# First block of a two-layer product on one core: halves of k for two strips, and four strips ahead of the second half of x

## The chip, the cores and the metric

The kernel runs on one core of a Trainium2 chip. The metric is the device time of one execution in microseconds (us), the median of several runs. The engines are named as the profile names them: PE (matrix multiply), PEld (its weight load), DVE, ACT, POOL and SP. POOL, ACT and SP also start transfers (DMA).

## The reference

```python
def reference(x, w1, b1, w2):          # x 16x512x768, w1 768x3072, b1 3072, w2 3072x768
    y = np.matmul(x, w1) + b1
    y = np.maximum(y, 0)
    return np.matmul(y, w2)
```

The 16x512 rows of x are one matrix of 8192 rows.

## The kernel before

The rows of x are cut into 8 blocks of 1024, and the hidden width of 3072 into two halves. The 16 pairs of a block and a half are the iterations. Each iteration has a first stage (x by w1, bias, relu, giving y) and a second stage (y by w2, added into the output). Fifteen iterations use a fast product scheme that forms sums of tiles of x, w1, y and w2 on DVE and needs fewer products. Its first stages are line 1091 and its second stages line 1219.

The very first first stage can't do that, because w1 and x are still on their way. It is written plainly in `first_block` (line 1021) with products from `plain` (line 983), whose matmuls are line 995. It works on six strips of w1. A strip is 256 columns with all 768 rows, so six matrices of 128x256; it is held as two halves of k, each with three of the six. The name `strip` counts 0 to 5, `j` picks one of a strip's two column tiles of 128, and `m` picks the first or the second 512 rows of the block. So there are 24 products `plain(strip, j, m)`. With `parts=2` a product is done as two groups of 256 rows (`n` is 0 or 1), with six matmuls of 256 columns each; with `parts=1` it is six matmuls of 512 columns. `split=True` cuts work further into the two halves of k, for n = 0 only. Each product fills one PSUM bank, and ACT evicts it with bias and relu into y (line 1003).

The first 512 rows come as four plain transfers, two each from SP and ACT. PE turns them (line 935, fp32), and DVE and ACT copy the results into x (lines 943 and 941). Everything else comes by POOL's queue, which also converts to 16 bits. The order is written out in `prologue` (line 717): strip 0 in two halves of k, strips 1 and 2 whole (`load_strip`, line 688, transfer on line 694), the second 512 rows of x in two transfers of 256 rows (`load_x`, line 710, transfer on line 715), strips 3 to 5, twelve pieces of w2 (line 700), and the first half of the next block. The second 512 rows are turned by PE in two groups of two tiles (`turns(0, 1)`, `turns(2, 3)`), again on line 935.

The order of PE's work is that of the program text. All other engines' instructions are put in order by a planner (`Graph.run`, line 390), which simulates the whole kernel with a table of costs. `presets` (line 739) tells it when each loaded piece is taken to have landed. The table changes no wait: on the chip each instruction waits for its real operands. It does change the order in which DVE, ACT, POOL and SP take their instructions, and which PSUM bank a product gets. `Reg("ps", leaves=...)` tells the planner in which state a bank is left.

Of the kernel before, what the change touches and what calls it, by code (L numbers as in the profile page):

```python
# [129 lines left out]
LAST_PARTS = ((0, 0, 384, "ACT", "SP"), (1, 0, 384, "ACT", "ACT"))  # L130
LAST_DIRECT = (0, 1, 2, 3, 4, 5, 7)
LAST_POOL = (0, 1, 3)

X_FUSE = (3,)
Y_FUSE = (8, 12, 18, 20)
# [148 lines left out]
class Graph:  # L284
# [23 lines left out]
    def add(self, engine, ns, fn, reads=(), writes=(), due=None, lat=0.0, after=(), idle=False, dma=0.0,  # L308
            early=0.0, spare=0.0, port=False):
        t = Task()  # L310
        t.n, t.engine, t.ns, t.fn, t.lat, t.due, t.idle = (
            len(self.tasks), engine, max(ns / 1000.0 - self.OVER[engine], 0.0), fn, lat, due, idle)
        t.succ, t.ready, t.end, t.start, t.dma, t.early = [], 0.0, None, None, dma, early
        t.spare, t.port = spare, port
        deps = set(after)
        for key in reads:
            w = self.writer.get(key)
            if w is not None:
                deps.add(w)
        for key in writes:  # L320
            w = self.writer.get(key)
            if w is not None:
                deps.add(w)
            deps.update(self.readers.get(key, ()))
        for key in reads:
            self.readers.setdefault(key, []).append(t)
        for key in writes:
            self.writer[key] = t
            self.readers[key] = []
        t.deps = deps  # L330
        t.waits = len(deps)
        for d in deps:
            d.succ.append(t)
        t.regs = list(dict.fromkeys(k for k in (*reads, *writes) if isinstance(k, Reg)))
        for r in t.regs:
            r.left += 1
        t.pe = None
        if engine == "PE":
            t.pe = self.npe
            self.npe += 1  # L340
            self.last_pe = t
        self.tasks.append(t)
        return t
# [250 lines left out]
class Fast:  # L594
# [122 lines left out]
    def prologue(self):  # L717
        nc = self.nc
        for s in range(4):
            (nc.sync, nc.scalar)[s % 2].dma_start(out=self.s[:, s],  # L720
                                                  in_=self.xf[s * P:(s + 1) * P, :])
            if s == 1:
                self.load_bias()
        self.constants()
        self.load_strip(self.v1, 0, 0, 0, 2)
        self.load_strip(self.v1, 0, 0, 1)
        self.load_strip(self.v1, 0, 0, 2)
        self.load_x(0, 1, 2)
        for h in range(3):
            self.load_strip(self.v1, 0, 1, h)  # L730
        for q in range(4):
            for h in range(3):
                self.load_w2(self.v2, 0, h, q)
        self.load_x(1, 0)
        for _ in range(9):
            nc.tensor.matmul(self.ps[:, 7, 0:P], lhsT=self.ones, rhs=self.ones, start=True,
                             stop=True)

    def presets(self):
        g = self.g  # L740
        for t, at in enumerate((9.3, 11.3, 13.3, 19.9, 21.8, 23.8)):
            for k in range(2):
                g.preset(("w1", t // 3, 2 * (t % 3) + k), at - (0 if t or k else 0.9))
        for q in range(4):
            for h in range(3):
                for n in range(2):
                    g.preset(("w2", 2 * q + n, h), 24.8 + 3 * q + h)
        for s in range(4):
            g.preset(("xn", 4 + s), 15.2 if s < 2 else 17.2)
            g.preset(("xn", s), 39.5)  # L750
            g.preset(("rows", s), (5.3, 5.3, 7.2, 7.2)[s])
        g.preset("b1_rows", 6.0)
# [229 lines left out]

    def plain(self, strip, j, m, parts=1, split=False):
        gi, h = divmod(strip, 3)
        ps = Reg("ps", leaves=2 if parts == 1 else 0)
        nc = self.nc

        def product(n, k2s):
            cols = slice(n * self.QM, (n + 1) * self.QM) if parts == 2 else slice(0, 512)
            for k2 in k2s:  # L990
                for k in range(3):
                    a = 4 * m + k2
                    rhs = (self.x[:, a:a + 3:2, k, :] if parts == 1
                           else self.x[:, a + 2 * n, k, :])
                    nc.tensor.matmul(self.ps[:, ps.at[0], cols],  # L995
                                     lhsT=self.v1[:, gi, 2 * h + k2, k, j * P:(j + 1) * P],
                                     rhs=rhs, start=(k2 == 0 and k == 0),
                                     stop=(k2 == 1 and k == 2), skip_group_check=True)

        def evict():  # L1000
            n = 4 * h + 2 * gi + j
            i = 8 * m + 2 * gi + j
            nc.scalar.activation(
                out=self.y[:, i:i + 5:4, h * self.QM:(h + 1) * self.QM],
                in_=self.ps[:, ps.at[0], :].rearrange("p (a m) -> p a m", a=2),
                func=ACTF.Relu, bias=self.b1y[:, n:n + 1])

        def add(n, k2s):
            rows = (0, 1) if parts == 1 else (n,)
            self.g.add("PE", 650 * len(k2s) // parts, lambda: product(n, k2s),  # L1010
                       reads=[("x", 4 * m + 2 * r + k2, q) for r in rows for k2 in k2s
                              for q in range(2)] + [("w1", gi, 2 * h + k) for k in k2s],
                       writes=[ps])
        for n in range(parts):
            for k2s in ((0,), (1,)) if split and n == 0 else ((0, 1),):
                add(n, k2s)
                yield
        self.g.add("ACT", 692, evict, reads=[ps, "b1y"],
                   writes=[("y", (2 * m + r) * 4 + 2 * gi + j, h) for r in range(2)])

    def first_block(self):
        for s in range(4):
            self.add_transpose_first(0, s)
            if s == 1:
                tables = self.add_bias()
        tables(self.g.tasks[-2:])

        def turns(*tiles):
            for s in tiles:
                self.add_transpose_first(1, s)  # L1030

        def run(*products):
            for p in products:
                for _ in p:
                    pass

        a, b = [self.plain(0, j, 0, 2, True) for j in range(2)]
        for p in (a, b, a, b):
            next(p)
        run(a, b, *(self.plain(1, j, 0, 2) for j in range(2)), self.plain(2, 0, 0, 2))  # L1040
        turns(0, 1)
        run(self.plain(2, 1, 0, 2))
        late = [self.plain(strip, j, 1, 2) for strip, j in ((0, 0), (0, 1), (1, 0))]
        next(late[0])
        turns(2, 3)
        for p in late[1:]:
            next(p)
        run(*late, *(self.plain(strip, j, 1, 2) for strip, j in ((1, 1), (2, 0), (2, 1))))
        run(*(self.plain(strip, j, m) for strip in (3, 4, 5) for m in range(2) for j in range(2)))

    def y_keys(self, slot):
        return [("y", slot, h) for h in range(3)]
# [145 lines left out]
    def add_second(self, it):  # L1198
# [67 lines left out]
        def store(to, reg, plain):  # L1266
            out, rows = sum_of(reg), self.rows_of(it, to)
            if plain:
                nc.sync.dma_start(out=rows, in_=out)
            else:  # L1270
                nc.gpsimd.dma_start(out=rows, in_=out, accum_op=ALU.add)  # L1271
# [14 lines left out]
        def prior_task(t):  # L1286
            _, _, u, b, _, to, _ = SECOND_OPS[t]
            e, ns = ("POOL", 2400) if t in LAST_POOL else ("DVE", 955)
            if e == "POOL" and (t in LAST_HALVES or t in taken_by):
# [12 lines left out]
        for kind, n in steps:  # L1302
# [97 lines left out]
            if what == "out":  # L1400
                plain = c == 0 and n not in apart or direct
                self.g.add("SP" if plain else "POOL", 100 if plain else 1375,
                           lambda to=to, dest=dest, plain=plain: store(to, dest, plain),
                           reads=[dest], writes=[("out", self.block(it), to)],
                           lat=3.5 if direct else 9.0,
                           dma=1.09 if direct else 1.2 if plain else 2.45)
# [192 lines left out]
```

## Time and profile before

| | us |
|---|---|
| median of 3 runs | 847.02 |
| lowest and highest | 846.86 and 847.36 |
| the profiled execution | 847.05 |
| its span, first to last instruction | 845.4 |
| PE busy in that span | 839.2 |

The profile is of one execution. Times within it count from the span's start. Matmuls are pipelined: the length given for one reaches past the start of the next one, so the pace is read from how long a row of many takes. An engine's busy time is the union of its instructions. "Idle before" with an arrow names what ended the wait. The chain of work that ended last is followed back from the last instruction.

### The profile page before, as it was taken

To read this page: it belongs to the slowest core of one execution; us is meant where nothing else is said; L and a number is where in the kernel's file an instruction comes from. 1 tells how busy PE (TensorE), PEld (TensorE's weight loads), DVE (VectorE), ACT (ScalarE), POOL (GpSimd) and SP (SyncE) were. 2 spreads that over 40 slices of the span, in tenths; PEclk is the share of its full clock that TensorE was granted. 3 is DMA by queue.
4 is the path that set the end of the run, shared out by engine and by line. 5 is a ranking of instruction groups with operands and counts; after the bars stand their busy time and mean duration, and the time that the engine had idled before them with its cause. 6 is when DMAs were issued, how large, how long until landed. Compare 5 with 4: busy or idle time off the path is not lost.

```text
span 845.4 us, 16819 instructions
## 1 busy us (share of the span) xinstructions
PE 839.2 (99%) x6383; PEld 625.7 (74%) x6383; DVE 736.2 (87%) x1229; ACT 567.3 (67%) x1199; POOL 171.7 (20%) x185
## 2 busy tenths in 40 slices
PE   9999999999999999999999999999999999999997
PEld 8568778686786867768687686877868678686874
DVE  5899988969889697988999979798896979979787
ACT  4866876779677684856858568766757666456462
POOL 6210011102011010010030503224041230501303
PEclk9999999999999999999999999999999999999999
DMA  9997498978988678594893977979799797986926
GB/s 211 205 178 186 85 223 110 170 178 132 216 114 154 165 132 189 102 212 153 237 176 66 196 122 121 189 108 175 119 137 148 117 174 113 145 136 76 178 85 169
DMA packets 171111, 128.93 MB, mean 153 GB/s; under 512 B 93948, under 2 KB 169492, under 8 KB 171028
## 3 DMA queue, kind: packets, MB, share of 16 engines
q0 software_dynamic: 56576, 68.82, 53.2%
q1 hardware_dynamic: 113984, 58.02, 29.1%
q8 instruction: 50, 0.82, 0.4%
q10 hardware_dynamic: 468, 1.00, 0.3%
q14 instruction: 33, 0.27, 0.1%
HBM read 73.54 MB, written 69.21 MB: 169 GB/s over the span
## 4 chain that ended last, share of the span: by engine, by line
PE 98%; DMA 1%; POOL 0%; ACT 0%; DVE 0%; issue 0%; POOLq 0%; DVEq 0%; ACTq 0%
PE ps L1219 48%; PE ps L1091 47%; PE ps L995 4%; DMA v<-in_w_dram 1%; PE ps L935 0%; ACT s L1230 0%; POOL v L694 0%; DVE s L1236 0%; POOL ident masks.py:199 0%; POOL ident L667 0%; POOL high L679 0%; POOL low L680 0%; POOL ident masks.py:197 0%; PE ps L1417 0%; PE ps L1428 0%
## 5 line engine op out<-in xcount | busy, mean ns | idle before, releaser
L1219 PE MATMUL ps<-v,y 128*128 128x384 f16 x2496 | 408.2, 326 | 0.0
L1091 PE MATMUL ps<-x,v 128*128 128x256 f16 x3600 | 395.6, 273 | 0.0
L1091 PEld LDWEIGHTS <-v 128*128 128x128 f16 x3600 | 352.3, 98 | 42.2
L1219 PEld LDWEIGHTS <-y 128*128 128x128 f16 x2496 | 244.2, 98 | 159.9
L1230 ACT ACTIVATE s<-ps 128x384 f32<-128x384 f32 (+1 forms) x245 | 153.1, 643 | 125.2 <-PE ps L1219 118.9
L1063 DVE TENSOR_TENSOR y<-y 128x768 f16<-128x768 f16 (+1 forms) x384 | 219.4, 619 | 2.6
L1134 DVE CUSTOM_DVE_ANT_0 y<-ps,s 128x512 f16<-128x512 f32 x240 | 156.0, 686 | 52.8 <-ACT s L1131 39.8
L1271 POOL DMA_DIRECT2D out_dram<-s x78 | 93.8, 1453 | 146.2 <-ACT s L1230 91.6
L1131 ACT ACTIVATE s<-ps,bt 128x256 f32<-128x256 f32 x180 | 75.2, 469 | 62.8 <-PE ps L1091 56.5
L838 DVE TENSOR_TENSOR x<-x 128x768 f16<-128x768 f16 (+1 forms) x210 | 113.6, 579 | 1.2
L1131 ACT ACTIVATE y<-ps,bt 128x256 f16<-128x256 f32 x180 | 69.4, 485 | 10.8 <-PE ps L1091 10.8
L1230 ACT ACTIVATE ps<-ps 128x384 f32<-128x384 f32 (+1 forms) x143 | 67.0, 507 | 6.6 <-PE ps L1219 2.8
L1236 DVE TENSOR_TENSOR s<-ps,s 128x768 f32<-128x768 f32 x74 | 70.6, 954 | 0.9
L715 POOL DMA_DIRECT2D xn<-in_x_dram x30 | 25.9, 864 | 211.8 <-DMA x<-xn 100.9
L1236 DVE TENSOR_TENSOR s<-s,ps 128x768 f32<-128x768 f32 x60 | 57.1, 952 | 2.1
L777 ACT ACTIVATE junk<-xn 128x768 f16<-128x768 f16 x64 | 53.9, 843 | 0.3
L1274 POOL DMA_DIRECT2D out_dram<-s x15 | 17.8, 1184 | 169.3 <-ACT s L1230 157.6
L1131 ACT ACTIVATE ps<-ps,bt 128x256 f32<-128x256 f32 x60 | 26.7, 445 | 32.4 <-PE ps L1091 31.4
L1127 ACT ACTIVATE ps<-ps 128x512 f32<-128x512 f32 x60 | 35.3, 588 | 4.4 <-DVE y L1134 3.5
L1142 DVE TENSOR_TENSOR s<-s,ps 128x512 f32<-128x512 f32 x30 | 20.6, 686 | 17.8 <-PE ps L1091 17.8
L995 PE MATMUL ps<-x,v 128*128 128x256 f16 (+1 forms) x216 | 32.0, 308 | 0.2 <-DMA v<-in_w_dram 0.2
L1137 DVE SCALAR_TENSOR_TENSOR s<-ps,bt,s 128x256 f32<-128x256 f32 x60 | 26.1, 476 | 4.4 <-PE ps L1091 4.4
(61 smaller groups left out, 310.7 us busy)
## 6 DMA issues: line engine op xcount, KB each, us to landing
out_dram<-s POOLq DMA_DIRECT2D x93, 384.0 KB, 8.8
out_dram<-s SPq DMA_DIRECT2D x69, 384.0 KB, 7.1
xn<-in_x_dram POOLq DMA_DIRECT2D x28, 768.0 KB, 9.9
v<-in_w_dram POOLq DMA_DIRECT2D x14, 192.0 KB, 8.2
x<-out_dram SPq DMA_DIRECT2D x14, 192.0 KB, 2.4
w1d<-in_w_dram POOLq DMA_DIRECT2D x6, 384.0 KB, 6.4
w2d<-in_w_dram POOLq DMA_DIRECT2D x12, 192.0 KB, 5.0
v<-w1d SPq DMA_DIRECT2D x12, 192.0 KB, 4.7
```

Of the source, the lines that this page charges most:

```text
L777: self.nc.scalar.activation(out=self.junk, in_=self.xn[:, s, :], func=ACTF.Square, accum_out=self.stat[:, self.stat_at["x"] + i:][:, 0:1])
L838: self.nc.vector.tensor_tensor(out=self.two(x, out), in0=self.two(x, in0), in1=self.two(x, in1), op=ALU.add if sign > 0 else ALU.subtract)
L995: nc.tensor.matmul(self.ps[:, ps.at[0], cols], lhsT=self.v1[:, gi, 2 * h + k2, k, j * P:(j + 1) * P], rhs=rhs, start=(k2 == 0 and k == 0), ...
L1063: self.nc.vector.tensor_tensor(out=self.two(self.y, out), in0=self.two(self.y, in0), in1=self.two(self.y, in1), op=ALU.add if sign > 0 els ...
L1091: nc.tensor.matmul(self.ps[:, at, j * self.QM:(j + 1) * self.QM], lhsT=self.v1[:, gi, self.w1s[c][gi][FIRST_V[p]], k, j * P:(j + 1) * P], ...
L1127: nc.scalar.activation(out=out, in_=ps, scale=float(a), func=func if kind == "out" else ACTF.Copy)
L1131: nc.scalar.activation(out=out[:, j], in_=ps[:, j], func=func, scale=float(a), bias=beta(j))
L1134: nc.vector._custom_dve(TENSOR_ADD_SAT, out=out, in0=ps, in1=s, s0=F_MAX, s1=0.0)
L1219: nc.tensor.matmul(self.ps[:, bank[ch].at[j], 0:NH], lhsT=self.y[:, ys[SECOND_U[p]], m0:m0 + P], rhs=self.v2[:, slot[SECOND_V[p]], h, :], ...
L1230: nc.scalar.activation(out=out, in_=ps, func=ACTF.Copy, scale=float(a))
L1236: engine.tensor_tensor(out=out, in0=in0, in1=in1, op=ALU.add if a == b else ALU.subtract)
L1271: nc.gpsimd.dma_start(out=rows, in_=out, accum_op=ALU.add)
```

## The change

Strip 1 is now loaded in two halves of k, as strip 0 was. Strips 2 and 3 follow whole, and only then the second 512 rows of x; strips 4 and 5 come after them. That is one transfer more in all.

On the first 512 rows PE now works strips 0 and 1 with both `j` interleaved: all four groups of three matmuls that need the first half of k, then the four that need the second. Strips 2 and 3 follow with matmuls of 512 columns. The last of their four products stands between the two groups of transposes. After that come the second 512 rows with strips 0 to 3; three products there are still done as 256 and 256 columns, the others with 512. Strips 4 and 5 end the block as before. `start` is set for a bank's first group only, and every bank is now left as full. The table of landings is set to other values.

```diff
+EARLY = 4
 ...
         self.load_strip(self.v1, 0, 0, 0, 2)
-        self.load_strip(self.v1, 0, 0, 1)
-        self.load_strip(self.v1, 0, 0, 2)
+        self.load_strip(self.v1, 0, 0, 1, 2)
+        for strip in range(2, EARLY):
+            self.load_strip(self.v1, 0, *divmod(strip, 3))
         self.load_x(0, 1, 2)
-        for h in range(3):
-            self.load_strip(self.v1, 0, 1, h)
+        for strip in range(EARLY, 6):
+            self.load_strip(self.v1, 0, *divmod(strip, 3))
 ...
-        for t, at in enumerate((9.3, 11.3, 13.3, 19.9, 21.8, 23.8)):
+        for t, at in enumerate((9.45, 11.45, 13.45, 15.45, 22.0, 24.0)):
             for k in range(2):
-                g.preset(("w1", t // 3, 2 * (t % 3) + k), at - (0 if t or k else 0.9))
+                g.preset(("w1", t // 3, 2 * (t % 3) + k), at - (0 if t > 1 or k else 0.9))
 ...
-                    g.preset(("w2", 2 * q + n, h), 24.8 + 3 * q + h)
+                    g.preset(("w2", 2 * q + n, h), 25.05 + 3 * q + h + (0.3 if 3 * q + h > 5 else 0))
 ...
-            g.preset(("xn", 4 + s), 15.2 if s < 2 else 17.2)
+            g.preset(("xn", 4 + s), 17.35 if s < 2 else 19.95)
 ...
-        ps = Reg("ps", leaves=2 if parts == 1 else 0)
+        ps = Reg("ps", leaves=2)
 ...
-                                     rhs=rhs, start=(k2 == 0 and k == 0),
+                                     rhs=rhs, start=(first and k2 == 0 and k == 0),
 ...
-        for n in range(parts):
-            for k2s in ((0,), (1,)) if split and n == 0 else ((0, 1),):
-                add(n, k2s)
-                yield
+        steps = [(n, k2s) for k2s in (((0,), (1,)) if split else ((0, 1),)) for n in range(parts)]
+        for i, (n, k2s) in enumerate(steps):
+            add(n, k2s, i == 0)
+            yield
 ...
-        a, b = [self.plain(0, j, 0, 2, True) for j in range(2)]
-        for p in (a, b, a, b):
-            next(p)
-        run(a, b, *(self.plain(1, j, 0, 2) for j in range(2)), self.plain(2, 0, 0, 2))
+        for strip in range(2):
+            pair = [self.plain(strip, j, 0, 2, True) for j in range(2)]
+            for p in 4 * pair:
+                next(p)
+            run(*pair)
+        early = [self.plain(strip, j, 0) for strip in range(2, EARLY) for j in range(2)]
+        run(*early[:-1])
         turns(0, 1)
-        run(self.plain(2, 1, 0, 2))
+        run(early[-1])
         late = [self.plain(strip, j, 1, 2) for strip, j in ((0, 0), (0, 1), (1, 0))]
 ...
-        run(*late, *(self.plain(strip, j, 1, 2) for strip, j in ((1, 1), (2, 0), (2, 1))))
-        run(*(self.plain(strip, j, m) for strip in (3, 4, 5) for m in range(2) for j in range(2)))
+        run(*late, self.plain(1, 1, 1),
+            *(self.plain(strip, j, 1) for strip in range(2, EARLY) for j in range(2)))
+        run(*(self.plain(strip, j, m) for strip in range(EARLY, 6) for m in range(2)
+              for j in range(2)))
```

## Rows read from the trace of the kernel before

**Rows 1.** The page's head, busy times by engine, and the chain's shares by engine.

```profile
span 845.4 us, 16819 instructions
PE 839.2 (99%) x6383; PEld 625.7 (74%) x6383; DVE 736.2 (87%) x1229; ACT 567.3 (67%) x1199; POOL 171.7 (20%) x185
PE 98%; DMA 1%; POOL 0%; ACT 0%; DVE 0%; issue 0%; POOLq 0%; DVEq 0%; ACTq 0%
```

**Rows 2.** Chain that ended last, in order of time: start us, us, what.

```profile
3.29 6.20 DMA v<-in_w_dram
9.50 0.05 issue
9.54 6.07 PE ps L995 x54
15.61 0.67 PE ps L935 x12
...
41.75 25.35 PE ps L1219 x156
67.10 26.20 PE ps L1091 x240
...
427.95 26.34 PE ps L1091 x240
...
815.43 24.39 PE ps L1219 x150
```

**Rows 3.** Timeline of PE, 5.4 to 9.6 us: start, us, line, shape, count.

```profile
8.56 0.82 PE L995 MATMUL ps<-x,v 128*128 128x256 f16 x6
9.54 0.28 PE L995 MATMUL ps<-x,v 128*128 128x256 f16 x1 [0.16 <-DMA v<-in_w_dram]
```

**Rows 4.** Timeline of PE in windows from 18.8, 26.4 and 36.2 us.

```profile
18.76 7.37 PE L995 MATMUL ps<-x,v 128*128 128x256 f16 x66
...
26.18 10.09 PE L995 MATMUL ps<-x,v 128*128 128x512 f16 x46
...
35.89 0.89 PE L995 MATMUL ps<-x,v 128*128 128x512 f16 x3
```

**Rows 5.** POOL's transfers one by one from 2.35 us: KB written, us to landing.

```profile
v<-in_w_dram POOLq DMA_DIRECT2D x1, 192.0 KB, 6.1
v<-in_w_dram POOLq DMA_DIRECT2D x1, 192.0 KB, 6.2
v<-in_w_dram POOLq DMA_DIRECT2D x1, 384.0 KB, 7.4
v<-in_w_dram POOLq DMA_DIRECT2D x1, 384.0 KB, 8.5
xn<-in_x_dram POOLq DMA_DIRECT2D x1, 384.0 KB, 9.6
xn<-in_x_dram POOLq DMA_DIRECT2D x1, 384.0 KB, 11.5
v<-in_w_dram POOLq DMA_DIRECT2D x1, 384.0 KB, 12.8
```

**Rows 6.** Timeline of all engines, POOL's rows, 2 to 18.3 us.

```profile
2.35 3.41 POOL L694 DMA_DIRECT2D v<-in_w_dram  x4
5.75 1.43 POOL L715 DMA_DIRECT2D xn<-in_x_dram  x2
7.15 2.51 POOL L694 DMA_DIRECT2D v<-in_w_dram  x3
...
18.21 0.71 POOL L700 DMA_DIRECT2D v<-in_w_dram  x1 [1.81 <-DMA xn<-in_x_dram]
```

**Rows 7.** Timeline of DVE in windows from 8.45 and from 11 us.

```profile
8.50 0.56 DVE L943 CAST x<-ps 128x384 f16<-128x384 f32 x1
...
31.92 7.22 DVE L872 TENSOR_TENSOR v<-v 128x1152 f16<-128x1152 f16 x10 [0.63 <-ACT v L862]
39.10 10.15 DVE L1063 TENSOR_TENSOR y<-y 128x768 f16<-128x768 f16 x17
```

More of the change, by code (lines that the diff above doesn't have):

```diff
@@ L984, in plain, with product @@
         gi, h = divmod(strip, 3)
-        ps = Reg("ps", leaves=2 if parts == 1 else 0)
+        ps = Reg("ps", leaves=2)
         nc = self.nc
-        def product(n, k2s):
+        def product(n, k2s, first):
             cols = slice(n * self.QM, (n + 1) * self.QM) if parts == 2 else slice(0, 512)
@@ L1006, in evict, with add @@
                 func=ACTF.Relu, bias=self.b1y[:, n:n + 1])
-        def add(n, k2s):
+        def add(n, k2s, start):
             rows = (0, 1) if parts == 1 else (n,)
-            self.g.add("PE", 650 * len(k2s) // parts, lambda: product(n, k2s),
+            self.g.add("PE", 650 * len(k2s) // parts, lambda: product(n, k2s, start),
                        reads=[("x", 4 * m + 2 * r + k2, q) for r in rows for k2 in k2s
```

## The prediction

> **What bounds the kernel now.** I read the page's head and the chain's shares first. PE is busy 839.2 of 845.4 us, and the chain that ended last is 98% PE [rows 1]. So the question for any edit is how much of PE's line is not matmuls at full pace. The chain in order of time answers it [rows 2]. From 41.75 us on, second stages of 25.35 us alternate with first stages of 26.20, and only one stage stands out, the 26.34 us at 427.95. The reader should see that nothing behind 41.75 has anything to give: a gain there arrives only as an earlier start. The end, 845.4 less 839.8 where the last products stop, is eviction and store, which the change leaves alone.
>
> The stretch that the change touches is line 995. For pace I take rows of many matmuls: 66 of 256 columns take 7.37 us, and less the 0.27 that the last one runs on, (7.37 - 0.27) / 65 = 0.109 us each; 46 of 512 columns give (10.09 - 0.38) / 45 = 0.216 [rows 4]; a group of twelve 16-bit transposes takes 0.67 [rows 2]. The block has 144 of the first, 72 of the second and two such groups: 144 x 0.1092 + 72 x 0.2158 + 2 x 0.67 = 15.72 + 15.54 + 1.34 = 32.60 us. The block runs from 8.56 [rows 3] to 41.58, when the first matmul of the next stage starts (the chain puts it at 41.75, since it counts the last matmul's run-on of 0.16 to the block [rows 2]). That is 33.02 us, so 0.42 us is lost.
>
> Two rows hold it. Six matmuls start at 8.56 and the next at 9.54 [rows 3]; six at full pace would end at 8.56 + 0.655 = 9.21, so 0.33 is lost waiting for the second half of strip 0 (the row's own 0.16 starts only after the run-on). And three matmuls take 0.89 at 35.89 [rows 4], where 2 x 0.216 + 0.38 = 0.81 is the pace: 0.08 of issue, with no transfer in it. **So the whole prize is the 0.33 us.**
>
> **The change part by part.**
>
> *Halves of k first.* At 8.56 PE now has four groups of three for the first half, for n = 0 and n = 1 and both j: 12 x 0.109 = 1.31 us, to 9.87. The second half lands at 3.29 + 6.2 = 9.49 [rows 2, 5]. The wait goes: -0.33. What is late next is the copy of x for n = 1, needed at 9.21. It is DVE's last copy, 8.50 + 0.56 = 9.06 [rows 7]. No row shows how fast PE follows such a copy; the nearest is the landing that PE followed in 0.05 [rows 2]. I take 0.05, so it fits with 0.10 to spare, and keep 0 to 0.33 as its ends.
>
> *Fewer, longer matmuls.* Strip 2 (both m) and the product of strip 1, j = 1, m = 1 turn from 60 matmuls of 256 into 30 of 512: 60 x 0.1092 - 30 x 0.2158 = 6.55 - 6.47, -0.08. All of it is on PE's line. PE should count 6383 - 30 = 6353.
>
> *One more transfer.* POOL's issues take about 0.85 us each [rows 6], far ahead of the data: strip 3 is issued at 7.15 and lands at 19.95 [rows 5, 6]. So the extra issue is hidden by the transfers queued ahead. In the transfer stream it might cost more. Landings now: 8.45, 9.49, then 11.5, 13.4, 15.35, 17.95 (an issue at 6.45 plus 11.5; the release on POOL at 18.21 agrees) and 19.95 [rows 5, 6]. A half strip came 1.04 behind its other half, a whole strip 1.9 to 2.0 behind the one before; half of that is 0.98, so an extra transfer costs 0.06. The high end is the second part of x, which came 2.6 behind the first where a strip of the same size takes 1.95: 0.65 more, with the same bytes. I take 0.06, the row of the very same kind of load.
>
> The Trainium skill speaks against this split: its page "DMA: Bandwidth & Descriptors", section "Anatomy of one DMA", gives each transfer of this path about 2.0 us fixed plus its bytes by bandwidth. In the stream that would put everything behind strip 1 two us later. The rows show the half 1.04 us behind its twin, so here loads that queue overlap that cost; no run shows it alone yet.
>
> *The new order against the landings.* With the pace above and the stream's steps (half 1.04, whole 1.95, second part of x 2.6):
> - strip 1: halves needed at 11.18 and 12.49, landed about 10.5 and 11.5;
> - strip 2: needed at 13.80, landed 13.5;
> - strip 3: needed at 13.80 + 12 x 0.2158 = 16.39, landed 15.4;
> - first part of x: needed at 17.68, landed 17.35;
> - second part of x: needed at 17.68 + 0.67 + 1.295 + 0.655 = 20.31, landed 19.95.
>
> The thinnest covers are 0.3 to 0.36 us. Behind that, 30 matmuls of 256 and five products of 512 bring PE to 20.31 + 0.67 + 3.28 + 6.48 = 30.73, when strip 4 is long there (its issue follows strip 3's by one, so about 22). Strips 4 and 5 end it: 30.73 + 8 x 1.295 + the 0.08 of issue = 41.17, against 41.58. Difference **-0.41**, the same as -0.33 - 0.08.
>
> *What the earlier end runs into.* The next stage wants sums from DVE. The first y sums start at 39.10, 0.60 each (10.15 / 17), and no product waited [rows 2, 7]. The first product at 41.58 had 41.58 - 39.65, about 1.9 us of cover; the following ones come every 0.975 us (25.35 / 26), slower than the sums. Now PE comes 0.4 earlier and w2 at most 0.55 later by the new table, which leaves about 1 us. Two y sums that stood near 26 us need strips 0 to 2 of the second rows, which now end near 28; DVE has sums of w1 to do meanwhile. Evictions stay 24, one per product; the full banks change only which bank is taken. Cost: 0, with 1 us of cover.
>
> **The sum.** 847.05 for the profiled execution less 0.41 is 846.64. The median, 847.02, lies 0.03 below that execution: **846.6**.
>
> **Rivals.**
> 1. *The change removes nothing*: the copy for n = 1 comes too late, and PE waits up to the same 0.33 at 9.21 instead of 9.21 to 9.54. For: only 0.15 us between the copy's end and the need. Against: 0.05 was enough for a landing. Time 847.02 - 0.08 = 846.9.
> 2. *Late stream*: the extra transfer costs its high end, 0.65. Then strip 2 lands at 14.1 and PE waits 0.3 at 13.80; everything behind is late by as much and still meets its data. Time 846.6 + 0.3 = 846.9.
> 3. *Each load pays its own start*: a load would begin only when the one before is done. The first load took 6.1 from an issue of 0.85 [rows 5, 6], so 5.25 behind it, of which 0.98 is data by the stream's pace: a start of up to 4.3. Strip 2 then lands 4.3 later, PE waits 4.3 - 0.3 = 4.0, and the time is 846.6 + 4.0 = 850.6. Against: whole loads land every 1.95 us, less than such a start. By the rule of the page named above the start is 2.0, the wait 1.7 and the time 848.3.
> 4. *Slower: the new landing table reorders the whole kernel.* DVE is busy 87% [rows 1], and the planner lays out all its instructions from the table. In before only one of 31 later stages lost 0.14 (26.34 against 26.20 [rows 2]). If the new order left that in every stage, 31 x 0.14 = 4.3 us: 846.6 + 4.3 = 850.9. It decides (slower by 0.2%, 1.69 us) from (1.69 + 0.41) / 0.14 = 15 stages on. Against: 30 of 31 are at PE's pace, with room in DVE's cover, and shifts of half a microsecond enter only at the start.
>
> **How the numbers follow.** The measurement can tell about 0.2%, 1.7 us, from no change; all of the prize is 0.05%. The forecast gets 0.74, rival 1 0.11, rival 2 0.08, rival 3 0.01, rival 4 0.04. The last 0.02 is a gain I can't see, in the tail of some 5 us behind the last product or in the front of 8.56 us, which the change doesn't touch. Same: 0.74 + 0.11 + 0.08 = 0.93; slower 0.01 + 0.04 = 0.05; faster 0.02. The range: down, the issue gap of 0.08 and the stage's 0.14 may close, 846.4, and the three runs before lie 0.16 below their median at the lowest, 846.2; up, rivals 1 and 2 at 846.9 to 847.0, and the runs lie 0.34 above at the highest, 847.35. So 846.2 to 847.4.
>
> **What would show it.** In the profile after: PE x6353; no gap of PE between 8.56 and 9.87, else rival 1 (a wait for DVE's copy at 9.21); no wait for a transfer at 13.80, 17.68 or 20.31, else rival 2 or 3; the second stage in the chain from about 41.35 instead of 41.75; the stages behind at 25.35 and 26.20, else rival 4. The prediction is wrong if the time leaves the range, and its reason is wrong if the gap at 9.2 goes and PE's start of the next stage doesn't move by 0.3 to 0.45 us.

## The result and the profile after

The change makes the kernel slower: 849.06 us (848.46 to 850.68) against 847.16 (846.86 to 847.65), a ratio of 1.0023 with an interval of 1.0016 to 1.0030. The profiled execution took 849.62 us with a span of 848.0, so it lies 0.56 above its median.

The page's head and PE's part of the busy times come first; they answer [rows 1].

```profile
span 848.0 us, 16760 instructions
PE 840.0 (99%) x6353; PEld 623.8 (74%) x6353; DVE 736.4 (87%) x1229; ACT 567.4 (67%) x1199; POOL 172.5 (20%) x186
```

PE has the 6353 matmuls foreseen and is still busy 99%. Next the chain in order of time, which answers [rows 2] (start us, us, what):

```profile
...
5.68 2.37 PE ps L938 x12
8.21 1.46 PE ps L938 x12
9.67 9.12 PE ps L998 x66
18.80 0.67 PE ps L938 x12
...
42.20 25.35 PE ps L1227 x156
67.55 26.20 PE ps L1099 x240
...
545.04 13.26 PE ps L1099 x120
558.30 25.35 PE ps L1227 x156
...
816.34 24.88 PE ps L1227 x153
```

Then the timeline's rows on PE from 5.68, to be read beside [rows 3], and its last rows on ACT, SP's queue and ACT's queue (start, us, engine, line, shape, count):

```profile
5.68 2.37 PE L938 MATMUL ps<-ident,s 128*128 128x128 f32 x12 [0.17 <-DMA s<-in_x_dram]
...
9.51 9.29 PE L998 MATMUL ps<-x,v 128*128 128x256 f16 x66
18.63 0.83 PE L938 MATMUL ps<-ident,xn 128*128 128x128 f16 x12
...
841.24 1.04 ACT L1238 ACTIVATE s<-ps 128x384 f32<-128x384 f32 x2 [5.34 <-PE ps L1227]
841.27 1.33 SPq L1271 DMA_DIRECT2D out_dram<-s  x3
842.31 0.36 ACTq L1271 DMA_DIRECT2D out_dram<-s  x1
```

Cut into four pieces, the two profiled executions compare as follows. The *front* ends with the start of the first product, the *block* with the start of the first matmul of the next stage, the *rest* with the start of the last matmul, and the *end* with the span. The starts are those of single matmuls in the trace.

| us | front | block | rest | end | span |
|---|---|---|---|---|---|
| before | 8.56 | 33.02 | 798.87 | 4.96 | 845.42 |
| after | 9.51 | 32.53 | 799.33 | 6.66 | 848.03 |
| difference | +0.95 | -0.50 | +0.46 | +1.70 | +2.61 |

The block did what it was meant to do. No gap is left at 9.2 us, and 66 matmuls of 256 and 512 columns run without one. The loss is elsewhere, above all behind PE's last matmul, in a stretch that no line of the change touches.

**What is in that end.** The view of transfers shows the last store of ACT (KB, us to landing). After, issued at 842.31:

```profile
out_dram<-s ACTq DMA_DIRECT2D x1, 192.0 KB, 4.7
```

And before, issued at 841.40:

```profile
out_dram<-s ACTq DMA_DIRECT2D x1, 192.0 KB, 2.8
```

The store takes 1.9 us longer to land. The same view gives the queues of after from 844.5 to 845.7 us and from 845.7 to 847 (packets, MB, share of 16 engines). q10 is ACT's queue and q8 carries loads of instructions.

```profile
q10 hardware_dynamic: 39, 0.04, 9.5%
q14 instruction: 2, 0.02, 5.5%
q8 instruction: 1, 0.02, 5.1%
...
DMA packets 8, 0.01 MB, mean 8 GB/s; under 512 B 1, under 2 KB 8, under 8 KB 8
q10 hardware_dynamic: 8, 0.01, 3.5%
```

One packet of 16 KB runs on q8 from 844.71 for 0.98 us. ACT's store is 144 packets, nine for each of the 16 transfer engines. Its last nine start only from 845.67 on, when that load is over, and run one behind the other, while the other 135 are done by 844.75. So they are one engine's share, and it waited for the load; no row names the engine. In before the last q8 packet stands in the window from 836.5 to 837.6, ahead of most of the last stores:

```profile
q8 instruction: 1, 0.02, 5.4%
```

The theory (R) follows: the 60 instructions of PE that the change saves (30 matmuls, 30 weight loads) move a load of PE's own instructions into the last store.

### The profile page after: what moved, and what is told of

Its sections match the earlier page's. It is cut to its first block, busy times and chain, and to the rows that moved or that the text cites. A ratio compares the mean times of both kernels' runs of the same rounds, so it can differ in the third digit from the quotient of the medians.

```text
span 848.0 us, 16760 instructions
## 1 busy us (share of the span) xinstructions
PE 840.0 (99%) x6353; PEld 623.8 (74%) x6353; DVE 736.4 (87%) x1229; ACT 567.4 (67%) x1199; POOL 172.5 (20%) x186
## 4 chain that ended last, share of the span: by engine, by line
PE 85%; issue 5%; DVE 5%; DMA 3%; ACT 1%; POOL 0%; DVEq 0%; ACTq 0%; POOLq 0%
PE ps L1227 42%; PE ps L1099 39%; PE ps L998 4%; DMA out_dram<-s 3%; DVE y L1071 1%; DVE y L1142 1%; DVE v L875 1%; PE ps L938 1%; DVE s L1244 1%; DMA s<-in_x_dram 1%; POOL out_dram L1279 0%; DVE x L841 0%; ACT s L1139 0%; ACT junk L889 0%; DVE s L1145 0%
## 5 line engine op out<-in xcount | busy, mean ns | idle before, releaser
L998 PE MATMUL ps<-x,v 128*128 128x512 f16 (+1 forms) x186 | 31.7, 331 | 0.0
```

What stands on the lines that cost most here:

```text
L998: nc.tensor.matmul(self.ps[:, ps.at[0], cols], lhsT=self.v1[:, gi, 2 * h + k2, k, j * P:(j + 1) * P], rhs=rhs, start=(first and k2 == 0 an ...
```

## The experiments

Besides R there were two rivals: D, the extra transfer or the new order of loads disturbs the transfers; C, everything is the slower start of PE (two thirds of the first twelve transposes ran at half pace, 0.213 us each, in 5.68 to 8.05).

### e_long: the long matmuls alone

```diff
 # before, with:
-        run(a, b, *(self.plain(1, j, 0, 2) for j in range(2)), self.plain(2, 0, 0, 2))
+        run(a, b, *(self.plain(1, j, 0, 2) for j in range(2)), self.plain(2, 0, 0))
         turns(0, 1)
-        run(self.plain(2, 1, 0, 2))
+        run(self.plain(2, 1, 0))
 ...
-        run(*late, *(self.plain(strip, j, 1, 2) for ...
+        run(*late, *(self.plain(strip, j, 1) for ...
```

> The kernel before with one part of the change alone: the five products of strip 2 and of strip 1, j = 1, m = 1 as six matmuls of 512 columns. Transfers, order and table stay as before; PE has 6353 instructions instead of 6383, as with the whole change. Theory R (the end is longer because PE's shorter program moves one 16 KB load of instructions to 844.7 us, where it holds one transfer engine for 1 us just as the last store runs): the load shows up again near 844 to 845 us, the stretch behind PE's last matmul is 6.6 us instead of 5.0, and the time is 1.6 less 0.1 us longer than before, about 848.6. Theory D (the end is longer because of the extra transfer and the new order of loads): the end stays at 5.0 us and the time is 0.1 us under before, 847.0. Theory C (all is the slower clock under the first transposes): the time is as before unless the granted clock is low there.

Measured: 848.91 us (848.55 to 849.26) against 847.05, ratio 1.0021 (1.0011 to 1.0030). PE's last load of instructions started at 843.35, and the end was 6.45 us. Nothing but the shape of 60 matmuls differs from before (DVE, ACT, POOL and SP keep their order), and nearly the whole loss is here. The rest of its span was 798.87, as before. The end holds 1.49 of the 1.83 us by which the span exceeds before's. The others are the front and the block: in this execution PE waited 0.32 us for rows of x at 8.37.

### e_order: all but the long matmuls

```diff
 # after, with:
-        early = [self.plain(strip, j, 0) for strip in range(2, EARLY) for j in range(2)]
+        early = [self.plain(strip, j, 0, 2 if strip == 2 else 1)
+                 for strip in range(2, EARLY) for j in range(2)]
 ...
-        run(*late, self.plain(1, 1, 1),
-            *(self.plain(strip, j, 1) for strip in range(2, EARLY) for j in range(2)))
+        run(*late, self.plain(1, 1, 1, 2),
+            *(self.plain(strip, j, 1, 2 if strip == 2 else 1)
+              for strip in range(2, EARLY) for j in range(2)))
```

> The whole change except for the 512 columns of those five products: they stay at 256, so PE has 6383 instructions as before, while the order of loads, the extra transfer, the halves of k and the table are those of the change. Theory R: the load of instructions lies near 837 us again, the end is 5.0 us, the first block saves its 0.33 us, and the time is 846.8 to 847.3 (the latter with the gap of 0.39 us near 544 us). Theory D: the end is 6.6 us as after the change, and the time about 849. Theory C: as after the change where the clock is low under the first transposes, up to 0.9 us more.

Measured: 847.16 us (846.82 to 847.57) against 847.05, ratio 1.0000 (0.9991 to 1.0009). Last load at 836.76, end 4.98 us, rest 798.87. In this execution ACT's last store landed in the old time:

```profile
out_dram<-s ACTq DMA_DIRECT2D x1, 192.0 KB, 2.8
```

So D falls for the end. C falls too: the first product started at 9.09, late too, and the time is that of before. And e_less24 (below) loses 1.5 us with a first product at 8.50, earlier than in before. But the 0.33 us of the removed wait are missing as well; that is taken up below.

### e_split: one transfer more, nothing else

```diff
 # before, with:
-        self.load_strip(self.v1, 0, 0, 1)
+        self.load_strip(self.v1, 0, 0, 1, 2)
```

> The kernel before with strip 1 loaded in two transfers and nothing else: one more POOL transfer, all instructions of PE, DVE, ACT and SP in place. Theory R: no change, 847.2, with the end at 5.0 us. Theory D: the end grows towards 6.6 us. For the gap of PE near 544 us (0.39 us, where a product waited for DVE, DVE for ACT, and ACT for a store on POOL's queue): if the extra transfer shifts POOL's queue, the gap is here too and costs 0.3 us; if it belongs to the instruction loads, it is not.

Measured: 847.60 us (847.35 to 848.08) against 847.05, ratio 1.0006 (0.9997 to 1.0015). The end is 4.98, and no gap stands at 544 us, so neither belongs to the extra transfer. POOL's releases by the two parts of x come at 15.57 and 18.27, where before has 15.69 and 18.21: one transfer more alone makes the stream no later, and rival 3 is not seen. The rest was 799.29 in this execution, with small gaps near 230 and 433 to 436 us that no other run shows. The interval holds no change; whether the 0.5 us is real stays open, but e_order and e_back60, with the same extra transfer, show none of it.

### e_plus24 and e_minus24: the load set to other places

```diff
 # e_plus24: after, with (24 instructions of PE more)
-        run(*(self.plain(strip, j, m) for strip in range(EARLY, 6) for m in range(2)
-              for j in range(2)))
+        run(*(self.plain(strip, j, m, 2 if (strip, m) == (5, 1) else 1)
+              for strip in range(EARLY, 6) for m in range(2) for j in range(2)))
 # e_minus24: before, with (24 instructions of PE less)
-        run(self.plain(2, 1, 0, 2))
+        run(self.plain(2, 1, 0))
 ...
-        run(*late, *(self.plain(strip, j, 1, 2) for strip, j in ((1, 1), (2, 0), (2, 1))))
+        run(*late, *(self.plain(strip, j, 1, 2) for strip, j in ((1, 1), (2, 0))),
+            self.plain(2, 1, 1))
```

> The whole change, and in addition two products of strip 5 done as 256 and 256 columns, so that PE has 12 matmuls and 12 weight loads more than after the change (6365). It adds 0.03 us of matmul work. Theory R: the last load of instructions comes about 0.09 us earlier for each instruction of PE put back, so near 841 to 842 us, before most of the last stores' data: the end is between 5.0 and 6.0 us, the time 0.6 to 1.6 us below that after the change, 847.5 to 848.5. Theory D or C: no change against the whole change, 849.

Measured: 848.39 us (847.65 to 849.11), ratio 1.0015 (1.0006 to 1.0024). A miss in the place: the load came at 837.57, some four microseconds earlier than worked out, and the end was 6.01.

> The kernel before with only two of its products (strip 2, j = 1, both m) as 512 columns: 24 instructions of PE less, nothing else. Theory R, now with the place of the load: the last load of instructions moves from 836.6 us by about 24 x 0.09 = 2.2 us to about 838.8, into the stretch from 837 to 844 us where the last stores keep the transfer engines full. The end grows from 5.0 to 6.0 us and the time by about 1.0 us, 848.0 to 848.4. If the load only harms where it meets the very last store (843 us on), the time is that of before, 847.0 to 847.2.

Measured: 848.38 us (847.90 to 848.79) against 847.15, ratio 1.0014 (1.0005 to 1.0023). The load came at 838.67, the end was 6.40. This is the kernel before with 12 matmuls fewer, and it loses 1.2 us. SP's queue (q1) around the load shows why the place matters (packets, MB, share of 16 engines). In e_order, 836.7 to 837.7 us:

```profile
q1 hardware_dynamic: 69, 0.10, 29.7%
```

In e_plus24, 837.5 to 839 us:

```profile
q1 hardware_dynamic: 353, 0.52, 97.3%
```

In e_minus24, 838.6 to 839.7 us:

```profile
q1 hardware_dynamic: 263, 0.38, 98.2%
```

From 836.7 to 837.7 SP's queue uses 30% of the engines, and the engine with the load catches up. From 837.5 on the last stores fill them to 97 or 98%, and what one engine loses there, it doesn't win back: in e_plus24 eight packets of SP's last store run one behind the other from 844.76 to 845.25, when the stores' other packets are done.

The traces also show what sets the place. Counted in single starts, the last load begins when PE has started 12693 to 12719 of its matmuls and weight loads, in all ten kernels with more than 12706 of them. An edit changes how many are left by then: 47 in before, 37 in e_plus24, 27 in e_minus24. Why it was 12693 in e_plus24 and 12715 in e_minus24, so that the load came sooner in the kernel with 12 instructions less, was not settled.

### e_back60 and e_less24: the count restored elsewhere, and lowered further

```diff
 # e_back60: after, with (60 instructions of PE more)
-        run(*(self.plain(strip, j, m) for strip in range(EARLY, 6) for m in range(2)
-              for j in range(2)))
+        run(*(self.plain(strip, j, m, 2 if strip == 5 or (strip, j, m) == (4, 1, 1) else 1)
+              for strip in range(EARLY, 6) for m in range(2) for j in range(2)))
 # e_less24: after, with
-        for _ in range(9):
-            nc.tensor.matmul(self.ps[:, 7, 0:P], lhsT=self.ones, rhs=self.ones, ...
+        wide = self.ones[:, 0:1].to_broadcast([P, 4 * P])
+        for n in (4, 4, 1):
+            nc.tensor.matmul(self.ps[:, 7, 0:n * P], lhsT=self.ones, rhs=wide[:, 0:n * P], ...
```

> The whole change, and five products of strips 4 and 5 (which the change doesn't touch) done as 256 and 256 columns, so that PE has the 6383 instructions of before. Theory R: it is the count that matters and not which products are long: the last load of instructions is near 837 us, the end 5.0 us, and the time 846.9 to 847.3, some 1.9 below the whole change. Rival: if it were the long matmuls of strip 2 themselves, or the order, the time stays near 849.

Measured: 847.11 us (846.93 to 847.61) against 847.21, ratio 0.9999 (0.9990 to 1.0008). Load at 837.03, end 4.94. This is the whole change, with the 60 instructions put back in five products that it never touched, and the loss is gone. It is the count.

> The whole change with the nine warm-up matmuls as three wide ones of the same total length: 24 instructions of PE less than after the change, 84 less than before. Theory R: the last load would be due about 2.2 us after the 844.7 us seen after the change, when the last store is done, or doesn't come at all within the kernel: the end is back at 5.0 to 5.5 us and the time at 846.8 to 847.5. If fewer instructions as such were the harm, the time is 849 or more. Theory L besides: the first load comes near 17 us, the release behind the first part of x near 17.7.

Measured: 848.69 us (848.25 to 849.62), ratio 1.0020 (1.0011 to 1.0030). A miss: the load came at 842.60, not later than 844.7, and the end was 6.82. In the three kernels with 6353 matmuls or fewer (e_long, after, e_less24) the last matmul starts at 840.80, 841.37 and 840.10, and the load 2.5, 3.3 and 2.5 us behind it. They have 12706 instructions or fewer, no more than PE had started in most of the others when the load came. So a load that hasn't come by then is not put off; it comes with the end of the program. That is also why the place worked out for e_plus24 was wrong: it was counted back from after's load, which came by the end and not by the count.

The Trainium skill's page "Runtime: NRT & Kernel Launch", section "Instruction fetch mechanics", says that an engine's instructions arrive in blocks of 16 KiB, 256 instructions, over a queue of the sequencer's own, and that a taken branch to a place not yet loaded forces a load. The traces agree: q8's packets are 16384 bytes, there are 50 in before, and PE's 2 x 6383 instructions are 49.9 blocks of 256. A branch stands at the program's end, 0.9 to 1.0 us behind the last matmul's start in before and after. That page of the Trainium skill also calls the cost of crossing into the next block "mostly hidden". Here a block costs 1.2 to 1.9 us of the median where it meets the last stores, and the measurement decides. That the branch is what asks for the load at 842.6 to 844.7 fits: it takes 0.31 us in these three kernels and 0.18 to 0.19 in the other ten. It was not tried apart.

### e_early and e_later: the same load in the first block

In e_order POOL's issues, which wait for landings in turn, show what became of the 0.33 us. The timeline's rows of POOL for before have the release by the second part of x at 18.21 [rows 6] and by the first at 15.69:

```profile
15.69 0.71 POOL L700 DMA_DIRECT2D v<-in_w_dram  x1 [1.23 <-DMA xn<-in_x_dram]
```

Those of e_order:

```profile
15.73 0.71 POOL L702 DMA_DIRECT2D v<-in_w_dram  x1 [1.27 <-DMA v<-in_w_dram]
18.52 0.72 POOL L702 DMA_DIRECT2D v<-in_w_dram  x1 [2.08 <-DMA xn<-in_x_dram]
20.39 0.71 POOL L702 DMA_DIRECT2D v<-in_w_dram  x1 [1.16 <-DMA xn<-in_x_dram]
```

Of e_early:

```profile
16.73 0.71 POOL L702 DMA_DIRECT2D v<-in_w_dram  x1 [2.13 <-DMA v<-in_w_dram]
18.30 0.72 POOL L702 DMA_DIRECT2D v<-in_w_dram  x1 [0.86 <-DMA xn<-in_x_dram]
20.18 0.71 POOL L702 DMA_DIRECT2D v<-in_w_dram  x1 [1.16 <-DMA xn<-in_x_dram]
```

And of e_later:

```profile
15.78 0.72 POOL L702 DMA_DIRECT2D v<-in_w_dram  x1 [1.24 <-DMA v<-in_w_dram]
17.67 0.72 POOL L702 DMA_DIRECT2D v<-in_w_dram  x1 [1.17 <-DMA xn<-in_x_dram]
20.33 0.72 POOL L702 DMA_DIRECT2D v<-in_w_dram  x1 [1.95 <-DMA xn<-in_x_dram]
```

In e_order it is the *first* part of x that takes 2.8 us behind strip 3, not the second. PE's first load of instructions stands at 15.58 there, at 16.02 in after and at 15.46 in before, where the second part was the next to land. Theory L says that this load makes the piece slow; rival S, that it is the piece's place in the stream.

```diff
 # e_early: e_order, with
-        for _ in range(9):
+        for _ in range(6):
 ...
+        ones16 = self.ones.bitcast(FP16)
+        for _ in range(16):
+            nc.tensor.matmul(self.ps[:, 7, 0:P], lhsT=ones16[:, 0:P], rhs=ones16[:, P:2 * P], ...
 # e_later: e_order, with the three wide warm-up matmuls of e_less24,
 #          and plain(5, j, 1) as parts=2, so that the later loads stay in place
```

> As e_order (the change with five products left at 256 columns), and three of the nine fp32 matmuls that warm PE up before the rows of x are there become sixteen short 16-bit ones, about as long together. PE has 20 instructions more ahead of the first block, so each load of instructions comes earlier; the first one, seen at 15.6 us, at about 14.5. Theory L (that 16 KB load holds one transfer engine for 1 us and so delays by 0.65 us whichever piece is under way; with the changed order at 15.6 this is the first part of the second 512 rows of x, which PE needs at 17.7 where its work started at 8.5): the slow piece is now strip 3, landing near 16.1, and the first part of x is back near 17.5: POOL's release that follows it comes at 17.7 instead of 18.5, PE's wait ahead of the transposes goes, and the next stage starts 9.12 + 23.45 = 32.6 us after the first product wherever that starts. Median 0.1 to 0.4 under e_order, 846.8 to 847.05. Rival S (the first part of x is slow by its own place in the stream): POOL's release stays at 18.5, the time at 847.15.

Measured: 846.91 us (846.80 to 847.28) against 847.15, ratio 0.9998 (0.9989 to 1.0007). The load came at 14.40, and the slow piece is now strip 3 (16.73, was 15.73). The first part of x itself takes 1.57 instead of 2.79 us, but strip 3 hands its delay on. So the release came back by only 0.2, to 18.30 instead of the expected 17.7, and PE still waited: its gap ahead of the transposes was 0.27.

> As e_order, with the nine warm-up matmuls as three wide ones of the same total length, so 24 instructions of PE less ahead of the first block, and 24 more put back in the two last products of strip 5 (256 columns), so the count is e_order's from there on. The first load of instructions comes later, at about 16.9 us, the last ones as in e_order. Theory L: the second part of x is the slow piece or shares it with the first; the release behind the first part of x comes at 17.7 to 18.2 and that behind the second at 20.4 to 20.7. The end is 5.0 us. Rival S: the releases stay at 18.5 and 20.4. Time 847.0 to 847.3 by either.

Measured: 846.94 us (846.57 to 847.51), ratio 0.9997 (0.9988 to 1.0006). The load came at 17.17, the release by the first part of x at 17.67, and the second part now takes 2.66. Which piece is slow moves with the load in both directions, as L says; S falls. PE has no gap in this block: it takes 32.63 us.

### e_five and e_five_early: more cover

```diff
 # e_five: e_order, with
-EARLY = 4
+EARLY = 5        (and the table set to match)
 # e_five_early: e_five with the warm-up of e_early
```

> As e_order, with five strips instead of four loaded and worked ahead of the second 512 rows of x (and the table set for it). The first part of x is then needed 2.6 us later and lands 1.95 us later, so the cover for it grows by 0.65 us. Theory L (or S): PE has no wait in the block at any start from 8.5 us on; the block takes 32.6 us, 0.1 to 0.6 us less than the same start gave in e_order, and the median is 846.7 to 847.0. If the block shows a new wait for the second part of x or for DVE's sums behind it, the time is 847.2 or more.

Measured: 846.97 us (846.45 to 847.78), ratio 1.0000 (0.9991 to 1.0009). The block is 32.60 us with a first product at 8.47, where e_plus24 (8.51) needed 33.18 and e_back60 (8.50) 33.53. The cover does what was expected for the block. The median moved by 0.2 at most; the profiled execution, at 846.45, is the fastest of the eleven.

> e_five with the warm-up of e_early (20 instructions of PE more): first load of instructions near 14.4 us, where strip 3 has room for it, the last near 833 us, ahead of the last stores, where e_early had an end of 4.8 us. It should be the fastest so far: 846.6 to 846.95 against 847.15, if the early load costs PE no wait for strip 3 or 4.

Measured: 846.75 us (846.33 to 847.40) against 847.21, ratio 0.9994 (0.9985 to 1.0003). It is the lowest median, and its interval still holds no change.

All the runs beside each other (times of single starts from the traces; "load" is PE's last load of instructions):

| | median us | ratio (95%) | PE matmuls | load at | end |
|---|---|---|---|---|---|
| before | 847.16 | | 6383 | 836.61 | 4.96 |
| after | 849.06 | 1.0023 (1.0016 to 1.0030) | 6353 | 844.71 | 6.66 |
| e_long | 848.91 | 1.0021 (1.0011 to 1.0030) | 6353 | 843.35 | 6.45 |
| e_less24 | 848.69 | 1.0020 (1.0011 to 1.0030) | 6341 | 842.60 | 6.82 |
| e_plus24 | 848.39 | 1.0015 (1.0006 to 1.0024) | 6365 | 837.57 | 6.01 |
| e_minus24 | 848.38 | 1.0014 (1.0005 to 1.0023) | 6371 | 838.67 | 6.40 |
| e_split | 847.60 | 1.0006 (0.9997 to 1.0015) | 6383 | 836.99 | 4.98 |
| e_order | 847.16 | 1.0000 (0.9991 to 1.0009) | 6383 | 836.76 | 4.98 |
| e_back60 | 847.11 | 0.9999 (0.9990 to 1.0008) | 6383 | 837.03 | 4.94 |
| e_five | 846.97 | 1.0000 (0.9991 to 1.0009) | 6383 | 835.94 | 4.92 |
| e_later | 846.94 | 0.9997 (0.9988 to 1.0006) | 6383 | 836.46 | 4.95 |
| e_early | 846.91 | 0.9998 (0.9989 to 1.0007) | 6393 | 832.98 | 4.79 |
| e_five_early | 846.75 | 0.9994 (0.9985 to 1.0003) | 6393 | 833.24 | 4.81 |

Every kernel whose load lies at 837.03 or before has an end of 4.8 to 5.0 us; every one from 837.57 on has 6.0 to 6.8.

## Why the prediction was wrong

**The step that failed: "The end ... is eviction and store, which the change leaves alone."** It leaves every instruction of the end alone, but not its time: 4.96 became 6.66 us. The prediction counted the 30 matmuls that fall away only as 0.08 us of matmul work, and never asked what else their number sets. It sets where in time PE's instructions are fetched. The page of before names these loads (q8, 50 of 16 KB), and I read no row of them. e_long gives the price of that one edit, forecast as -0.08: +1.86 us.

**Rival 4 had the right sign and the wrong cause.** It put the loss into a new order of the instructions in all stages. But from 40 us on DVE, ACT, POOL and SP take the same instructions in the same order in before and after. Ahead of that, the places of some of DVE's sums and copies and of ACT's evictions differ. PSUM bank numbers differ up to some 400 us, which moves no start. Nine of the eleven experiments have a rest of 798.87 to 798.88 us, as before has. After's 799.33 comes from single gaps, the 0.39 ahead of 545.04 the largest, in a product that waited for DVE, ACT and a store on the way; e_less24 has one of 0.20 near 410. Since e_order, e_plus24 and e_back60, with the same transfers and order of loads, have neither, I count them to single executions; the cause stays open.

**The landing of x was wrong in place.** The step "second part of x 2.6" took a fault of the moment for a property of the piece. The load of instructions near 15.5 us makes slow whatever is then under way (e_early, e_later), and in the new order that is the first part. It landed at about 18.2 to 18.5 where 17.35 was forecast and 17.68 was the need, so the cover of 0.33 was none: e_plus24 and e_back60, which started early, lost 0.62 and 0.91 us there. The wait shows on the timeline of PE for e_plus24:

```profile
18.25 0.84 PE L938 MATMUL ps<-ident,xn 128*128 128x128 f16 x12 [0.45 <-DMA xn<-in_x_dram]
```

The forecast's rival 2, "late stream", is this, with another price and reason.

**The front was taken as fixed.** The prediction started PE at 8.56. In the profiled executions of the 13 kernels the first product starts anywhere from 8.47 to 9.51, with a front of the same instructions in most of them (the last section has what moves it). In before, a start up to 8.88 costs nothing, because the second half of strip 0 is late anyway: e_split started at 8.89 and had no wait there at all. So the 0.33 us are partly a cushion. Taking the wait away gives little in an execution that starts late, and this, with the late x, is why e_order is no faster than before.

**What was right.** The pace (0.109 and 0.216), 6353 matmuls, no wait for DVE's copy (rival 1), the transfer in halves at no cost that PE saw (rival 3: no landing moved by microseconds), the cover of DVE's sums behind the block, and the block itself: 32.61 us forecast (41.17 less 8.56), 32.53 to 32.64 where x was in time. The further 0.08 in after is the issue gap at 36 us [rows 4], which isn't there.

For the median, then: of +1.9 us the end has 1.7 in the profiled execution, the first block gives back nothing on balance (e_order, e_back60), and the 0.2 left are within the scatter of the runs.

## What to carry to other kernels

Count an edit's instructions as well as its time: an unrolled program is fetched in blocks by the same transfer engines that move the data, and a change of a few dozen instructions anywhere moves all later fetches. Where stores or loads keep the engines full up to a deadline (the last store above all), look at the instruction queues' rows in that stretch, and compare two kernels at equal instruction counts before a change of a microsecond is put down to anything else. A slow piece in a stream is a property of the piece only if it stays slow when the order changes, and a wait that absorbs a scattered start is worth less than its length.

## What was not expected of the hardware

- A load of 16 KB of instructions, the first or the last of a kernel, held one transfer engine for 0.9 to 1.4 us and delayed the data under way: the first part of x by 0.85 us (18.52 against 17.67), the last store by 1.9 us (4.7 against 2.8).
- With 30% use of the engines around it (e_order) a load cost nothing at the end; at 97% (e_plus24) it cost 1.0 us.
- Removing 24 instructions of 12766 from PE made the kernel 1.2 us slower (e_minus24).
- PE's first transposes ran at 0.213 us each for a while in some executions (after: twelve in 2.37 us) and at 0.109 in others (before: twelve in 1.50 us), with the same instructions ahead of them. The pace is that of 1.2 GHz against 2.4. The profile's granted clock reads 1.00 in both stretches, but the trace's first record of the clock, the full one, begins at 5.57 us in before and only at 7.46 in after, just where the pace changes. So the column has no record ahead of that to go by. Of the six kernels that start their first product at 8.89 or later, five have that record at 6.30 to 7.46, and the sixth, e_long, waited for rows of x. The others have it at 4.14 to 5.99. Twelve transposes in 2.37 instead of 1.50 us account for most of the 0.95 us by which the first product of after starts later; why the clock rises later in some executions stays open.
